# A log-sum-exp kernel on one core: hand-placed semaphores, a four-row first load ahead of the opening barrier, and 18 loads in place of 17

## The chip, the core and the metric

The kernel runs on one core of a Trainium2 chip. The metric is the device time of one execution in microseconds (us). The profile's span, from the program's first instruction to its last, is about 1.8 us shorter than that time. ScalarE, VectorE, GpSimd and SyncE run programs of their own and tell each other of finished work through semaphores, which are counters. At the start and the end of a program all of them wait for each other; these are the opening and the closing barrier. Loads are issued by SyncE and carried out by 16 transfer engines, called "the engines" below where loads are spoken of. A difference in a profile is given in us of the span; a difference between kernels in the runs is given as a ratio, with its us beside it.

## The reference

```python
x = randn(32, 512, 1024).astype(float32)           # axis = -1
x_max = max(x, axis=-1, keepdims=True)
out = x_max.squeeze(-1) + log(sum(exp(x - x_max), axis=-1))    # 32 x 512 float32
```

The input is 67.1 MB. Each of the 16,384 rows of 1,024 numbers gives one number. Both kernels leave the maximum out: with inputs of this size exp does not overflow. The 16,384 rows lie as 128 on each of the 128 partitions, so "a row" below means one row on all 128 partitions, 512 KB.

## The kernel before

A load brings r rows into a ring of 50 row slots. ScalarE takes the exponential in place. The sums go two ways: for the first `n_dve` rows of a load ScalarE takes the exponential in one long instruction and VectorE sums; for the others ScalarE does the row and its sum in one instruction with an accumulator. Logarithms follow in small pieces, and one store ends the kernel. The framework places all semaphores.

```python
CHUNKS = [                                    # (rows, rows summed on VectorE)
    (15, 8), (16, 8), (16, 8), (16, 8), (14, 9), (11, 8), (9, 6), (7, 5), (5, 4),
    (5, 3), (4, 3), (3, 2), (2, 1), (2, 2), (1, 0), (1, 0), (1, 0),
]
RING_ROWS = 50
LN_FROM = 4
# ... cut: pool, tiles, table load ...
    row = slot = logged = 0
    for i, (r, n_dve) in enumerate(CHUNKS):
        if slot + r > RING_ROWS:
            slot = 0
        nc.sync.dma_start(out=ring[:, slot : slot + r], in_=x_v[:, row : row + r])
        if i == len(CHUNKS) - 1:
            take_logs(logged, row)            # a logarithm ahead of the last row
            logged = row
        if n_dve:
            nc.scalar.activation(out=ring[:, slot : slot + n_dve], in_=..., func=Exp)
            nc.vector.reduce_sum(out=sums[:, row : row + n_dve], in_=..., axis=AX)
        for j in range(n_dve, r):
            nc.scalar.activation(out=ring[:, slot + j], in_=..., func=Exp,
                                 accum_out=sums[:, row + j : row + j + 1])
        if r >= LN_FROM:
            take_logs(logged, row)
            logged = row
        slot += r
        row += r
    take_logs(logged, NB)
    nc.scalar.dma_start(out=out_v, in_=res)
```

Loads are numbered from 0 in this text.

The softmax here doesn't subtract the row's maximum and nothing guards it: scores larger than these inputs give would overflow.

Of the kernel before, what the change touches and what calls it, by code (L numbers as in the profile page):

```python
# [1 line left out]

# [4 lines left out]



CHUNKS = [  # L10
    (15, 8), (16, 8), (16, 8), (16, 8), (14, 9), (11, 8), (9, 6), (7, 5), (5, 4),
    (5, 3), (4, 3), (3, 2), (2, 1), (2, 2), (1, 0), (1, 0), (1, 0),
]
RING_ROWS = 50

LN_FROM = 4


@with_exitstack
def kernel(  # L20
    ctx: ExitStack,
    tc: tile.TileContext,
    x: bass.AP,
    axis: bass.AP,
    out: bass.AP,
):
    nc = tc.nc
    P = nc.NUM_PARTITIONS

    assert axis in (-1, len(x.shape) - 1), f"only last-axis reduction supported, got {axis}"  # L30

    x_flat = x.flatten_outer_dims()
    N, D = x_flat.shape
    assert N % P == 0
    NB = N // P
    assert sum(r for r, _ in CHUNKS) == NB

    fp32 = mybir.dt.float32
    Exp = mybir.ActivationFunctionType.Exp
    Ln = mybir.ActivationFunctionType.Ln  # L40
    AX = mybir.AxisListType.X

    x_v = x_flat.rearrange("(p t) d -> p t d", p=P)
    out_v = bass.AP(tensor=out.tensor, offset=out.offset, ap=[[NB, P], [1, NB]])

    pool = ctx.enter_context(tc.tile_pool(name="pool", bufs=1))
    ring = pool.tile([P, RING_ROWS, D], fp32, name="ring")
    sums = pool.tile([P, NB], fp32, name="sums")
    res = pool.tile([P, NB], fp32, name="res")

    nc.scalar.preload_act_table_set("natural_log_exp_and_others")  # L51
    ctx.enter_context(tc.manual_schedule())

    def take_logs(lo, hi):
        if hi > lo:
            nc.scalar.activation(out=res[:, lo:hi], in_=sums[:, lo:hi], func=Ln)  # L56

    row = slot = logged = 0
    for i, (r, n_dve) in enumerate(CHUNKS):
        if slot + r > RING_ROWS:  # L60
            slot = 0
        nc.sync.dma_start(out=ring[:, slot : slot + r], in_=x_v[:, row : row + r])  # L62
        if i == len(CHUNKS) - 1:
            take_logs(logged, row)
            logged = row
        if n_dve:
            nc.scalar.activation(  # L67
                out=ring[:, slot : slot + n_dve], in_=ring[:, slot : slot + n_dve], func=Exp
            )
            nc.vector.reduce_sum(  # L70
                out=sums[:, row : row + n_dve], in_=ring[:, slot : slot + n_dve], axis=AX
            )
        for j in range(n_dve, r):
            nc.scalar.activation(  # L74
                out=ring[:, slot + j],
                in_=ring[:, slot + j],
                func=Exp,
                accum_out=sums[:, row + j : row + j + 1],
            )
        if r >= LN_FROM:  # L80
            take_logs(logged, row)
            logged = row
        slot += r
        row += r

    take_logs(logged, NB)
    nc.scalar.dma_start(out=out_v, in_=res)


# [1 line left out]
_INS = ['x', 'axis']  # L91
_OUTS = [((32, 512), 'float32')]

_NUMBERS = {'axis': -1}


# [26 lines left out]
```

## Time and profile before

The time is 166.47 us (median of 3 runs, 165.97 to 166.50). The profiled run took 166.17 us with a span of 164.4 us.

| what | before |
|---|---|
| first load issued by SyncE | 0.73 us |
| first load (15 rows) landed | 21.88 us |
| reload at the wrap of the ring issued | 57.00 us |
| last load landed | 159.82 us |
| ScalarE starts the last row | 160.51 us |
| store landed | 163.48 us |
| end of the span | 164.40 us |

Landings are times at which the sixteenth transfer engine has raised the load's semaphore, read from the trace's semaphore events.

The profile views in this document show chosen lines word for word; lines between them are left out, also where no dots stand. The view by stretches of the kernel before; the columns are the stretch, its length, busy time of VectorE, ScalarE and GpSimd with counts, granted clock, mean busy share of the 16 transfer engines, and GB/s:

```profile
4.00:60.00 56.00, 17.37 (x2) 29.76 (x33) 0.00 (x0) 1.00 1.01 435
60.00:80.00 20.00, 8.69 (x1) 15.45 (x18) 0.00 (x0) 1.00 0.99 427
80.00:140.00 60.00, 38.86 (x5) 57.09 (x53) 0.00 (x0) 1.00 0.99 426
```

The transfer engines are busy throughout, so the loads bound the middle.

The timeline of the opening of the kernel before (start, duration, engine, line, operation, tiles, count):

```profile
0.33 0.10 POOL L104 MEMSET const-uint8-127<- 128x1 uint8 x1
0.72 1.28 ACT L51 ACT_TABLE_LOAD   x1 [0.72 <-PEq L104]
0.73 1.32 SPq L62 DMA_DIRECT2D ring<-in_x_dram  x3
```

SyncE issues nothing before 0.73 us: until then the opening barrier holds it, GpSimd's constants being the last to finish.

The chain of work that ended last, of the kernel before (start, length, what):

```profile
1.15 40.05 DMA ring<-in_x_dram
...
48.29 8.70 DVE sums L70
...
57.00 0.33 SPq L62
...
57.37 40.16 DMA ring<-in_x_dram
...
158.01 2.30 DVE sums L70
...
160.33 0.02 ACTq L56
```

At 57.00 us SyncE issues reloads as soon as a sum on VectorE releases the slots. At 160.33 us a logarithm on ScalarE was waiting for VectorE's last sum. The timeline of the end of the kernel before:

```profile
158.01 2.29 DVE L70 TENSOR_REDUCE sums<-ring 128x2 f32<-128x2048 f32 x1 [1.14 <-ACT ring L67]
158.92 1.04 ACT L74 ACTIVATE ring<-ring 128x1024 f32<-128x1024 f32 x1
159.87 0.19 ACT L74 ACTIVATION_READ_ACCUMULATOR ring<-ring 128x1 f32 x1
160.39 0.21 ACT L56 ACTIVATE res<-sums 128x13 f32<-128x13 f32 x1 [0.34 <-DVE sums L70]
160.51 1.04 ACT L74 ACTIVATE ring<-ring 128x1024 f32<-128x1024 f32 x1
161.67 0.20 ACT L56 ACTIVATE res<-sums 128x1 f32<-128x1 f32 x1
161.91 0.37 ACTq L87 DMA_DIRECT2D out_dram<-res  x1
```

The last row was in memory at 159.82 us, and ScalarE starts it at 160.51 us, 0.69 us late.

### The profile page before, as it was taken

To read this page: it belongs to the slowest core of one execution; us is meant where nothing else is said; L and a number is where in the kernel's file an instruction comes from. 1 tells how busy PE (TensorE), PEld (TensorE's weight loads), DVE (VectorE), ACT (ScalarE), POOL (GpSimd) and SP (SyncE) were. 2 spreads that over 40 slices of the span, in tenths; PEclk is the share of its full clock that TensorE was granted. 3 is DMA by queue.
4 is the path that set the end of the run, shared out by engine and by line. 5 is a ranking of instruction groups with operands and counts; after the bars stand their busy time and mean duration, and the time that the engine had idled before them with its cause. 6 is when DMAs were issued, how large, how long until landed. Compare 5 with 4: busy or idle time off the path is not lost.

```text
span 164.4 us, 243 instructions
## 1 busy us (share of the span) xinstructions
DVE 82.0 (50%) x14; ACT 124.2 (76%) x133; POOL 0.2 (0%) x4
## 2 busy tenths in 40 slices
DVE  0000000991029800596006940399398979996970
ACT  3000069980999729995399969999989999799993
POOL 0000000000000000000000000000000000000000
DMA  6998999899799979979999989999999999999950
GB/s 239 478 448 389 407 462 510 383 383 510 335 431 510 431 335 494 462 335 496 433 446 433 433 382 428 449 420 431 431 403 433 421 434 424 425 426 416 408 222 16
DMA packets 2593, 67.18 MB, mean 409 GB/s; under 512 B 288, under 2 KB 416, under 8 KB 800
## 3 DMA queue, kind: packets, MB, share of 16 engines
q1 hardware_dynamic: 2448, 67.11, 95.2%
q10 hardware_dynamic: 144, 0.07, 0.1%
q14 instruction: 1, 0.01, 0.0%
HBM read 67.11 MB, written 0.07 MB: 409 GB/s over the span
## 4 chain that ended last, share of the span: by engine, by line
DMA 65%; ACT 18%; DVE 13%; issue 1%; SPq 0%; ACTq 0%
DMA ring<-in_x_dram 65%; ACT ring L67 14%; DVE sums L70 13%; ACT ring L74 4%; SPq L62 0%; ACT res L56 0%; ACTq L56 0%
## 5 line engine op out<-in xcount | busy, mean ns | idle before, releaser
L70 DVE TENSOR_REDUCE sums<-ring 128x8 f32<-128x8192 f32 (+7 forms) x14 | 82.0, 5866 | 78.3 <-ACT ring L67 78.3
L67 ACT ACTIVATE ring<-ring 128x8192 f32<-128x8192 f32 (+7 forms) x14 | 66.8, 4770 | 36.6 <-DMA ring<-in_x_dram 36.5
L74 ACT ACTIVATE ring<-ring 128x1024 f32<-128x1024 f32 x53 | 55.1, 1040 | 0.0
L74 ACT ACTIVATION_READ_ACCUMULATOR ring<-ring 128x1 f32 x53 | 9.9, 187 | 0.0
L56 ACT ACTIVATE res<-sums 128x16 f32<-128x16 f32 (+8 forms) x12 | 2.4, 198 | 0.4 <-DVE sums L70 0.3
L51 ACT ACT_TABLE_LOAD x1 | 1.3, 1283 | 0.7 <-PEq L104 0.7
L104 POOL MEMSET const-bfloat16-1.0<- 128x1 bf16 x1 | 0.1, 102 | 0.0
L104 POOL MEMSET const-uint8-127<- 128x1 uint8 x1 | 0.1, 102 | 0.0
L104 POOL MEMSET const-float32-0.0<- 128x1 f32 x1 | 0.1, 99 | 0.2 <-issue 0.2
L104 POOL MEMSET const-float32-1.0<- 128x1 f32 x1 | 0.1, 99 | 0.0
## 6 DMA issues: line engine op xcount, KB each, us to landing
ring<-in_x_dram SPq DMA_DIRECT2D x1, 7680.0 KB, 21.1
ring<-in_x_dram SPq DMA_DIRECT2D x1, 7168.0 KB, 40.2
ring<-in_x_dram SPq DMA_DIRECT2D x1, 5632.0 KB, 34.3
ring<-in_x_dram SPq DMA_DIRECT2D x2, 2560.0 KB, 33.4
ring<-in_x_dram SPq DMA_DIRECT2D x1, 4608.0 KB, 44.9
ring<-in_x_dram SPq DMA_DIRECT2D x1, 3584.0 KB, 33.9
ring<-in_x_dram SPq DMA_DIRECT2D x1, 2048.0 KB, 31.8
ring<-in_x_dram SPq DMA_DIRECT2D x2, 1024.0 KB, 37.9
```

The costliest lines, as they stand in the source:

```text
L51: nc.scalar.preload_act_table_set("natural_log_exp_and_others")
L56: nc.scalar.activation(out=res[:, lo:hi], in_=sums[:, lo:hi], func=Ln)
L67: nc.scalar.activation(out=ring[:, slot : slot + n_dve], in_=ring[:, slot : slot + n_dve], func=Exp)
L70: nc.vector.reduce_sum(out=sums[:, row : row + n_dve], in_=ring[:, slot : slot + n_dve], axis=AX)
L74: nc.scalar.activation(out=ring[:, slot + j], in_=ring[:, slot + j], func=Exp, accum_out=sums[:, row + j : row + j + 1],)
L104: nc = _bacc.Bacc("TRN2", target_bir_lowering=False, num_devices=1)
```

## The change

Its intent: write the programs of the engines directly, with one semaphore per load, so that the first load can be issued ahead of the opening barrier. With it come a first load of only four rows, another split of the rows, a ring of 51 slots, two logarithms in place of twelve, and GpSimd in place of SyncE as the engine that waits for the store. The core of the diff:

```diff
 CHUNKS = [
-    (15, 8), (16, 8), (16, 8), (16, 8), (14, 9), (11, 8), (9, 6), (7, 5), (5, 4),
-    (5, 3), (4, 3), (3, 2), (2, 1), (2, 2), (1, 0), (1, 0), (1, 0),
+    (4, 0), (16, 10), (14, 13), (15, 4), (16, 7), (15, 6), (12, 9), (9, 6), (7, 5), (5, 4),
+    (4, 3), (3, 3), (2, 2), (2, 0), (1, 1), (1, 0), (1, 0), (1, 0),
 ]
-RING_ROWS = 50
+RING_ROWS = 51
-LN_FROM = 4
+LN_EARLY = 6
 ... (cut: tiles become plain allocations; a semaphore per load, act_done, dve_done, stored)
+    def load(i):
+        (s, row), r = place[i], CHUNKS[i][0]
+        act_wait = max(a for a, _ in busy[s : s + r])
+        dve_wait = max(d for _, d in busy[s : s + r])
+        if dve_wait:
+            nc.sync.wait_ge(dve_done, dve_wait)
+        if act_wait:
+            nc.sync.wait_ge(act_done, act_wait)
+        nc.sync.dma_start(out=ring[:, s : s + r], in_=x_v[:, row : row + r]).then_inc(
+            landed[i], 16
+        )
 ...
+    load(0)
+    n_early = len(body.instructions)
 ...
+        if i == len(CHUNKS) - LN_EARLY:
+            logged = place[i - 1][1]
+            take_logs(0, logged, *done_before[i - 1])
+        nc.scalar.wait_ge(landed[i], 16)
 ... (cut: exponentials and sums as before, each with its increment)
-    take_logs(logged, NB)
-    nc.scalar.dma_start(out=out_v, in_=res)
+    take_logs(logged, NB, dves, acts)
+    nc.scalar.wait_ge(act_done, acts)
+    nc.scalar.dma_start(out=out_v, in_=res).then_inc(stored, 16)
+    nc.gpsimd.wait_ge(stored, 16)
 ...
+    first.instructions = head[:at] + work[:n_early] + head[at:end] + work[n_early:] + head[end:]
```

The last line puts the first load in front of SyncE's part of the barrier (`at`) and the rest behind the barrier.

More of the change, by code (lines that the diff above doesn't have):

```diff
@@ L44 @@
     out_v = bass.AP(tensor=out.tensor, offset=out.offset, ap=[[NB, P], [1, NB]])
-    pool = ctx.enter_context(tc.tile_pool(name="pool", bufs=1))
-    ring = pool.tile([P, RING_ROWS, D], fp32, name="ring")
-    sums = pool.tile([P, NB], fp32, name="sums")
-    res = pool.tile([P, NB], fp32, name="res")
-    nc.scalar.preload_act_table_set("natural_log_exp_and_others")
-    ctx.enter_context(tc.manual_schedule())
-    def take_logs(lo, hi):
-        if hi > lo:
-            nc.scalar.activation(out=res[:, lo:hi], in_=sums[:, lo:hi], func=Ln)
@@ L58 @@
-    row = slot = logged = 0
-    for i, (r, n_dve) in enumerate(CHUNKS):
+    ring = nc.alloc_sbuf_tensor("ring", [P, RING_ROWS, D], fp32).ap()
+    sums = nc.alloc_sbuf_tensor("sums", [P, NB], fp32).ap()
+    res = nc.alloc_sbuf_tensor("res", [P, NB], fp32).ap()
+    landed = [tc.alloc_semaphore(f"landed{i}") for i in range(len(CHUNKS))]
+    act_done = tc.alloc_semaphore("act_done")
+    dve_done = tc.alloc_semaphore("dve_done")
+    stored = tc.alloc_semaphore("stored")
+    hook = nc.pop_inst_callback()
@@ L60 @@
+    symbolic, nc._always_lower_symbolic_ap = nc._always_lower_symbolic_ap, False
+    place = []
+    row = slot = 0
+    for r, _ in CHUNKS:
         if slot + r > RING_ROWS:
             slot = 0
-        nc.sync.dma_start(out=ring[:, slot : slot + r], in_=x_v[:, row : row + r])
-        if i == len(CHUNKS) - 1:
-            take_logs(logged, row)
-            logged = row
+        place.append((slot, row))
+        slot += r
+        row += r
+    busy = [(0, 0)] * RING_ROWS
+    acts = dves = 0
@@ new lines, in load, with take_logs @@
+    def load(i):
[9 more added lines that the diff above has]
+        )
+    def take_logs(lo, hi, dve_wait, act_wait):
+        nonlocal acts
+        nc.scalar.wait_ge(act_done, act_wait)
+        nc.scalar.wait_ge(dve_done, dve_wait)
+        nc.scalar.activation(out=res[:, lo:hi], in_=sums[:, lo:hi], func=Ln).then_inc(
+            act_done, 1
+        )
+        acts += 1
@@ new lines @@
+    body = nc.main_func.blocks[-1]
+    assert not body.instructions
+    load(0)
+    n_early = len(body.instructions)
+    nc.scalar.preload_act_table_set("natural_log_exp_and_others")
+    logged = 0
+    done_before = [(0, 0)]
+    for i, (r, n_dve) in enumerate(CHUNKS):
+        if i:
+            load(i)
+        s, row = place[i]
+        if i == len(CHUNKS) - LN_EARLY:
+            logged = place[i - 1][1]
+            take_logs(0, logged, *done_before[i - 1])
+        nc.scalar.wait_ge(landed[i], 16)
@@ L66 @@
         if n_dve:
             nc.scalar.activation(
-                out=ring[:, slot : slot + n_dve], in_=ring[:, slot : slot + n_dve], func=Exp
-            )
+                out=ring[:, s : s + n_dve], in_=ring[:, s : s + n_dve], func=Exp
+            ).then_inc(act_done, 1)
+            acts += 1
+            nc.vector.wait_ge(act_done, acts)
             nc.vector.reduce_sum(
-                out=sums[:, row : row + n_dve], in_=ring[:, slot : slot + n_dve], axis=AX
-            )
+                out=sums[:, row : row + n_dve], in_=ring[:, s : s + n_dve], axis=AX
+            ).then_inc(dve_done, 1)
@@ L73 @@
+            dves += 1
+            for j in range(n_dve):
+                busy[s + j] = (0, dves)
         for j in range(n_dve, r):
             nc.scalar.activation(
-                out=ring[:, slot + j],
-                in_=ring[:, slot + j],
+                out=ring[:, s + j],
+                in_=ring[:, s + j],
                 func=Exp,
                 accum_out=sums[:, row + j : row + j + 1],
-            )
-        if r >= LN_FROM:
-            take_logs(logged, row)
-            logged = row
@@ L83 @@
-        slot += r
-        row += r
-    take_logs(logged, NB)
-    nc.scalar.dma_start(out=out_v, in_=res)
+            ).then_inc(act_done, 1)
+            acts += 1
+            busy[s + j] = (acts, 0)
+        done_before.append((dves, acts))
+    take_logs(logged, NB, dves, acts)
+    nc.scalar.wait_ge(act_done, acts)
+    nc.scalar.dma_start(out=out_v, in_=res).then_inc(stored, 16)
+    nc.gpsimd.wait_ge(stored, 16)
+    sp = mybir.EngineType.SP
+    first = nc.main_func.blocks[0]
+    head, work = first.instructions, body.instructions
@@ L91 @@
+    at = next(k for k, i in enumerate(head) if i.engine == sp and i.opcode == "Drain")
+    end = next(k for k, i in enumerate(head) if i.opcode == "UnconditionalBranch")
+    first.instructions = head[:at] + work[:n_early] + head[at:end] + work[n_early:] + head[end:]
+    body.instructions = []
+    nc._always_lower_symbolic_ap = symbolic
+    nc.push_inst_callback(hook)
 _INS = ['x', 'axis']
```

## The prediction

> **What bounds the kernel now.** The loads. The page's transfers: 67.11 MB, 95% of the 16 engines' span; by stretches, 435 GB/s from 4 to 60 us and 419 to 427 GB/s from 60 to 156 us. The Trainium skill, "DMA: Bandwidth & Descriptors", section "Where 436 GB/s comes from", gives 435 GB/s as the ceiling of the fabric; this trace agrees: the middle can't shrink. The transfer records fit 1.203 us a row plus about 0.08 us a load (16 rows: 19.32 us; one row: 1.28 us). The two ends are left:
>
> - Front: the first load is issued at 0.73 us, after the opening barrier (SyncE is ready at 0.00 us). First packets follow 1.02 us later; the sixteenth engine starts at 3.40 us. Start-up: 3.0 us in all.
> - Back: the last load lands at 159.82 us. ScalarE is then late: it waited for VectorE's last sum (until 160.30 us), took a logarithm at 160.39 us, and starts the last row at 160.51 us, 0.69 us after landing. Then exponential and accumulator 1.14 us, logarithm 0.2 us, store 1.6 us (161.91 to 163.48 us), SyncE's waits and drains about 0.27 us until GpSimd sees it, closing barrier 0.64 us: 164.4 us. The measured time is about 1.8 us more.
>
> **What the change does.**
>
> 1. First load before the barrier: issue from 0.73 us to near 0.0 us. GpSimd reaches the barrier last (0.53 us), and one issue costs SyncE 0.37 us, so the barrier itself should not move. All landings come about 0.7 us earlier, fully on the critical path. The second load is issued at 0.73 us; the four rows last until about 6 us: no gap.
> 2. 18 loads for 17: +0.08 us.
> 3. Ring and split. With durations of the trace (exponential of n rows 0.853n+0.1 us on ScalarE, row with accumulator 1.039 us, VectorE 1.067n+0.15 us), I estimated the new order by arithmetic. Every reload is released 10 us or more before the queue runs dry (load 4 at about 47 us, needed near 60; load 5 at 70, needed near 80), so no DMA gap. ScalarE is hardly idle from about 100 us on; the early logarithm costs a stop of about 0.9 us at 152 us for VectorE. The last load lands near 159.2 us and ScalarE starts its row about 0.6 us late, much as now. VectorE ends near 159.6 us, no longer last.
> 4. Logarithms 12 to 2: off the path. Separate waits for landings: about 0.05 us each.
> 5. GpSimd waits for the store itself: SyncE's chain goes, about 0.1 us.
>
> Sum: -0.7 +0.08 -0.1, and about -0.1 for the tail's order: -0.8 us.
>
> **Prediction: 165.6 us** (before 166.47), 8 in 10 within 164.8 to 166.3. Faster by over 2%: 0.03; within 2%: 0.95; slower: 0.02.
>
> **What would show it.** Step 1: SyncE's first load issue in the first 0.1 us of the timeline, barrier's end still near 0.65 us, last landing about 159.2 us. Step 3: transfers at 435 GB/s with no gap between 4 and 156 us; ScalarE's last row starting 0.4 to 0.8 us after the last landing. Step 5: under 0.2 us between the store's landing and GpSimd's barrier step.
>
> **What would make it wrong.** The early issue delays the barrier or its packets start later than 1.02 us after it. ScalarE, hardly idle from 100 us, becomes the bound. Reloads that wait for VectorE, whose 13-row sum takes 14 us, could leave the queue empty near 60 or 80 us.

## The result

The kernel after took 164.50 us (median of 4 runs, 164.29 to 164.59) against 166.44 us (median of 4) for the kernel before. The ratio is 0.9888, with a 95% interval of 0.9867 to 0.9908. Ratios in this document are the mean time of one kernel's fast runs over that of the other's of the same rounds, so they are not quite the ratios of the medians quoted. The gain is 1.9 us; 0.8 us was predicted, and the measured time lies below the stated range of 164.8 to 166.3 us.

| what | before | after | difference |
|---|---|---|---|
| first load issued | 0.73 | 0.00 | -0.73 |
| last load landed | 159.82 | 158.51 | -1.31 |
| last row started, after its landing | 0.69 | 0.27 | -0.42 |
| last row's start to the end of the span | 3.89 | 3.97 | +0.08 |
| span | 164.40 | 162.75 | -1.65 |

The view by stretches of the kernel after:

```profile
4.00:60.00 56.00, 15.74 (x2) 31.57 (x24) 0.00 (x0) 1.00 1.02 440
60.00:80.00 20.00, 13.43 (x2) 15.05 (x23) 0.00 (x0) 1.00 0.97 420
80.00:140.00 60.00, 31.85 (x5) 55.61 (x56) 0.00 (x0) 1.00 1.00 430
```

The bytes of these three stretches are within 1% of before's, as they must be when the engines are busy. Bytes are counted where a packet of up to 64 KB starts, so a stretch of 20 us can be off by a few per cent; landings are the finer measure.

The timeline of the opening of the kernel after:

```profile
0.00 2.41 SPq L82 DMA_DIRECT2D ring<-in_x_dram  x4
0.33 0.10 POOL L168 MEMSET const-uint8-127<- 128x1 uint8 x1
0.77 1.28 ACT L100 ACT_TABLE_LOAD   x1 [0.77 <-PEq L168]
```

The first issue now starts the span. The barrier ends 0.05 us later than before (ScalarE's table load moves from 0.72 to 0.77 us).

The chain of work that ended last, of the kernel after:

```profile
1.16 42.58 DMA ring<-in_x_dram
...
69.13 30.69 DMA ring<-in_x_dram
...
99.85 5.32 ACT ring L113
105.17 9.35 ACT ring L125 x18
114.52 7.78 ACT ring L113
...
122.33 29.26 DVE sums L118 x5
...
151.67 0.30 ACT res L90
```

From the landing of load 5 at 99.82 us the chain runs through ScalarE and VectorE, not through transfers. The timeline of its end:

```profile
157.74 1.04 ACT L125 ACTIVATE ring<-ring 128x1024 f32<-128x1024 f32 x1
158.69 0.18 ACT L125 ACTIVATION_READ_ACCUMULATOR ring<-ring 128x1 f32 x1
158.78 1.04 ACT L125 ACTIVATE ring<-ring 128x1024 f32<-128x1024 f32 x1
159.94 0.21 ACT L90 ACTIVATE res<-sums 128x11 f32<-128x11 f32 x1
160.18 0.37 ACTq L137 DMA_DIRECT2D out_dram<-res  x1
```

There is no logarithm between the rows. The last row starts 1.04 us after the one before it, the same pace as the rows with no wait at all, so ScalarE's own pace holds it, 0.27 us behind the landing at 158.51 us. The recorded 1.04 us of one exponential agrees with the Trainium skill, "ScalarE: Activation LUTs", section "What ACT_TABLE_LOAD costs", which gives 186 ns + 0.833 ns an element for an instruction whose scale and bias are immediates: 1039 ns for 1,024 elements. The pace is another matter: in this trace a row without accumulator is followed after 0.95 us (155.75 to 156.70 us), a row with one after 1.04 us.

### The profile page after: what moved, and what is told of

Its sections match the earlier page's. It is cut to its first block, busy times and chain, and to the rows that moved or that the text cites. A ratio compares the mean times of both kernels' runs of the same rounds, so it can differ in the third digit from the quotient of the medians.

```text
span 162.7 us, 208 instructions
## 1 busy us (share of the span) xinstructions
DVE 79.2 (49%) x13; ACT 123.2 (76%) x126; POOL 0.2 (0%) x4
## 4 chain that ended last, share of the span: by engine, by line
DMA 45%; DVE 27%; ACT 26%; issue 0%; SPq 0%; ACTq 0%
DMA ring<-in_x_dram 45%; DVE sums L118 27%; ACT ring L113 17%; ACT ring L125 9%; ACT res L90 0%; SPq L82 0%; ACTq L89 0%
## 5 line engine op out<-in xcount | busy, mean ns | idle before, releaser
L118 DVE TENSOR_REDUCE sums<-ring 128x4 f32<-128x4096 f32 (+9 forms) x13 | 79.2, 6138 | 79.0 <-ACT ring L113 79.0
L113 ACT ACTIVATE ring<-ring 128x4096 f32<-128x4096 f32 (+9 forms) x13 | 64.8, 4987 | 30.3 <-DMA ring<-in_x_dram 30.2
L125 ACT ACTIVATE ring<-ring 128x1024 f32<-128x1024 f32 x55 | 57.2, 1040 | 5.5 <-DMA ring<-in_x_dram 5.5
L90 ACT ACTIVATE res<-sums 128x117 f32<-128x117 f32 (+1 forms) x2 | 0.5, 256 | 0.4 <-DVE sums L118 0.4
```

What stands on the lines that cost most here:

```text
L90: nc.scalar.activation(out=res[:, lo:hi], in_=sums[:, lo:hi], func=Ln).then_inc(act_done, 1)
L113: nc.scalar.activation(out=ring[:, s : s + n_dve], in_=ring[:, s : s + n_dve], func=Exp).then_inc(act_done, 1)
L118: nc.vector.reduce_sum(out=sums[:, row : row + n_dve], in_=ring[:, s : s + n_dve], axis=AX).then_inc(dve_done, 1)
L125: nc.scalar.activation(out=ring[:, s + j], in_=ring[:, s + j], func=Exp, accum_out=sums[:, row + j : row + j + 1],).then_inc(act_done, 1)
```

## The experiments

The theory after the result: the landings came 1.31 us earlier and the tail was 0.42 us shorter because of four separate things, of which the prediction had sized only the first. They are (1) the issue ahead of the barrier; (2) the size of the first load; (3) a reload that the old split issues late at the wrap of the ring; (4) the logarithm that waits for VectorE ahead of the last row. The main rivals are that the programs themselves (without the framework's waits) gave the gain, that start-up shrank because the second issue comes later after the first, that one instruction fetch explains the excess of the landings, and that the new split of the rows gave it.

For the landings I use two derived numbers. "Start-up" is the time from the first issue to the first landing, less 1.203 us a row and 0.08 us. "Excess" is what the later landings take beyond 1.203 us a row and 0.08 us a load. All runs:

| run | ratio to before | first load, rows | issue | start-up | excess | last landing | last row late by |
|---|---|---|---|---|---|---|---|
| before | 1 | 15 | 0.73 | 3.01 | 0.70 | 159.82 | 0.69 |
| a1_own_only | 0.9999 | 15 | 0.73 | 3.12 | 0.81 | 160.04 | 0.72 |
| a2_own_hoist | 0.9960 | 15 | 0.00 | 3.03 | 1.11 | 159.52 | 0.70 |
| a3_own_hoist_small | 0.9935 | 4 | 0.00 | 2.70 | 1.05 | 159.21 | 0.69 |
| a5_wrap_fits | 0.9905 | 5 | 0.00 | 2.61 | 0.30 | 158.37 | 0.67 |
| a4_two_logs | 0.9904 | 4 | 0.00 | 2.42 | 1.20 | 159.08 | 0.19 |
| a6_wrap_and_logs | 0.9867 | 5 | 0.00 | 2.70 | 0.16 | 158.32 | 0.16 |
| after | 0.9888 | 4 | 0.00 | 2.59 | 0.46 | 158.51 | 0.27 |
| u1_load_behind | 0.9920 | 4 | 0.73 | 2.65 | 0.27 | 159.11 | 0.25 |
| u2_sync_waits | 0.9889 | 4 | 0.00 | 2.51 | 0.77 | 158.74 | 0.28 |
| u3_many_logs | 0.9886 | 4 | 0.00 | 2.54 | 0.85 | 158.85 | 0.35 |
| f1_few_scalar | 0.9959 | 4 | 0.00 | 2.59 | 0.12 | 158.17 | 1.77 |
| g1_extra_fetch | 0.9900 | 4 | 0.00 | 2.63 | 0.85 | 158.95 | 0.29 |
| r1_after_again | 0.9869 | 4 | 0.00 | 2.57 | 0.35 | 158.39 | 0.29 |
| r2_a6_again | 0.9870 | 5 | 0.00 | 2.73 | 0.10 | 158.29 | 0.16 |
| a7_last_on_time | 0.9865 | 5 | 0.00 | 2.60 | 0.18 | 158.24 | 0.13 |

The ratios have 95% intervals of 0.0012 to 0.0021 to either side, and each stands against runs of the kernel before on the same chip. The runs lie on several chips (a1 to a3 and u1 on one; a4, a5, u2 and u3 on a second; a6, f1 and g1 on a third; r1, r2 and a7 on a fourth), so a difference of two ratios is uncertain by 0.0018 to 0.003, which is 0.3 to 0.5 us. All results were correct. The other columns are of one profiled run each; the excess varies by a few tenths between runs of one kernel (0.46 and 0.35 for the kernel after). It was worked out with unrounded constants; with 1.203 and 0.08 the column is 0.03 to 0.04 us higher throughout.

### The programs alone, the issue, and the size of the first load

a1 is the kernel after with everything of the old schedule put back, so that only the engine programs, their semaphores and GpSimd's wait for the store remain:

```diff
-    (4, 0), (16, 10), (14, 13), ...
+    (15, 8), (16, 8), (16, 8), ...          # all 17 loads of before; ring of 50
-LN_EARLY = 6                                # and the twelve logarithms of before
+LN_FROM = 4
-    n_early = len(body.instructions)
+    n_early = 0                             # first load behind the barrier
```

> The engine programs with own semaphores alone: old 17 loads, old split, ring of 50, old twelve logarithms, first load behind the barrier; only the wait for the store is GpSimd's. Theory (the gain is made of an earlier issue, a smaller first load and a shorter tail): as the kernel before within 0.2 us, 166.3 us, first landing near 21.9 us, start-up (first issue to first landing, less 1.203 us a row and 0.08 us) 3.0 us. Rival (the programs themselves, without the framework's waits, are worth most of the 1.9 us): 165.3 us or less.

Measured: 166.44 us (166.35 to 166.49), ratio 0.9999. The programs with their own semaphores are worth nothing by themselves; that rival falls.

a2 is a1 with the first load of 15 rows ahead of the barrier.

```diff
-    n_early = 0
+    n_early = len(body.instructions)
```

> a1 with its first load of 15 rows ahead of the barrier. Theory (start-up depends on the size of the first load): issue 0.73 us earlier, start-up still 3.0 us, first landing 21.2 us, time 0.7 us under a1, about 165.6 us. Rival (start-up shrank by 0.4 us because the second issue then comes 0.78 us after the first instead of 0.42 us): start-up 2.6 us, first landing 20.7 us, time 1.1 us under a1.

Measured: 165.87 us (165.54 to 165.96), ratio 0.9960, so 0.65 us under a1. Start-up stayed at 3.03 us although the second issue now came 0.78 us after the first.

a3 is a2 with the first load cut in two.

```diff
-    (15, 8), (16, 8), ...
+    (4, 0), (11, 8), (16, 8), ...
```

> a2 with the first load cut into 4 and 11 rows (18 loads). Theory (size of the first load): start-up 2.6 us, first landing 7.5 us, second landing 0.35 us earlier than a2's first, time 0.3 us under a2, about 165.3 us. Rival (distance of the second issue): start-up as a2's, time as a2's or 0.08 us over.

Measured: 165.43 us (164.86 to 165.84), ratio 0.9935, 0.42 us under a2, with an uncertainty of about 0.4 us. Start-up fell to 2.70 us, and in the two profiles the last landing came 0.31 us earlier.

u1 takes the kernel after and puts only its first load back behind the barrier.

```diff
-    n_early = len(body.instructions)
+    n_early = 0
```

> The kernel after with its first load of four rows back behind the barrier, nothing else changed. Both theories: time 0.7 us over the kernel after, about 165.2 us, as all landings move by 0.73 us. They differ in the start-up: size of the first load says 2.6 us, distance of the second issue (now 0.42 us) says 3.0 us, and then the time is 1.1 us over the kernel after. If ScalarE's and VectorE's work from 100 us on were the bound on its own, not moved by landings, the time would stay at 164.5 us.

Measured: 165.13 us (164.95 to 165.26), ratio 0.9920, which is 0.53 us over the kernel after by its first ratio (0.9888) and 0.85 us by the repeated one (0.9869). Start-up was 2.65 us with the second issue 0.42 us after the first. Together a1, a2, a3 and u1 fill the two-by-two table:

| start-up in us | second issue 0.42 us later | second issue 0.78 us later |
|---|---|---|
| 15 rows | 3.12 (a1) | 3.03 (a2) |
| 4 rows | 2.65 (u1) | 2.59 (after), 2.70 (a3) |

The size of the first load sets the start-up, and the distance of the second issue does not. In the trace the first packets start 1.0 us after the issue in all these runs. With 15 rows the sixteenth engine starts between 1.2 and 1.7 us after the first one, with 4 rows 0.7 to 1.3 us after. These ranges overlap (1.16 us in a1, 1.33 us in u1), so the spread of the starts is not the whole of it. Why the size of the packets (60 KB against 16 KB) matters is not shown.

### The reload at the wrap of the ring

In the old split the first load has 15 rows, and load 3, the first to return to slot 0, has 16. It needs one slot of load 1 as well, and so waits for VectorE's sum of load 1. a5 moves one row, so that 16 slots are exactly two loads:

```diff
-    (4, 0), (11, 8), (16, 8), (16, 8), (16, 8), ...     # a3
+    (5, 0), (11, 8), (15, 8), (16, 8), (16, 8), ...
```

> a3 with one row moved: loads of 5, 11 and 15 rows in place of 4, 11 and 16. The first reload (16 rows, ring slots 0 to 15) then covers only the first two loads, as in the kernel after; in a3 it also covers one row of the third load and so is issued at 56.1 us, 3 us before its engines run dry at 59 us. Theory (a late reload at the wrap of the ring costs the old split 0.4 to 0.8 us, in idle engines and slow first packets near 59 us): reload issued near 38 us, no idle engine at 58 to 60 us, excess of the landings over 1.203 us a row falls from 1.05 us to 0.5 us or less, time 0.4 to 0.6 us under a3's 165.4 us. Rival (the excess is that of one instruction fetch near 74 us, or noise): excess stays near 1 us, time stays at 165.4 us.

Measured: 164.77 us (164.76 to 165.26), ratio 0.9905 against a3's 0.9935, 0.50 us less, with an uncertainty of about 0.4 us. The view of SyncE's issues and the view by stretches of a3:

```profile
56.11 0.80 SPq L82 DMA_DIRECT2D ring<-in_x_dram  x2
```

```profile
57.00:62.00 5.00, 0.00 (x0) 2.33 (x1) 0.00 (x0) 1.00 0.85 354
```

And the same two of a5:

```profile
37.83 18.46 SPq L82 DMA_DIRECT2D ring<-in_x_dram  x2
```

```profile
57.00:62.00 5.00, 0.00 (x0) 2.46 (x1) 0.00 (x0) 1.00 0.97 419
```

The reload is issued at 37.83 us instead of 56.11 us, and in the five microseconds around the wrap the engines are busy 97% instead of 85%. In a3's trace some engines have nothing to do from 58.4 us on, 0.36 us each on average and 1.91 us at most, and several packets there take 0.2 to 0.3 us longer; a5 has neither. The excess falls from 1.05 to 0.30 us.

In the kernel before the reload was issued at 57.00 us, 2.8 us before the first engine had landed its share of the load ahead of it (59.83 us). The view of the same stretch shows nothing of a loss:

```profile
57.00:62.00 5.00, 0.00 (x0) 1.25 (x1) 0.00 (x0) 1.00 1.04 446
```

The idle time there is 0.05 us on average over the 16 engines, but it is nearly all that of one engine, and that engine sets the landings. The trace doesn't name a packet's engine, but an engine's packets nearly always follow each other within 6 ns, so they can be put in rows by their starts. One engine ends its share of load 2 at 60.17 us and starts its share of load 3 only at 60.94 us. Its eight packets of 2.42 us then end at 80.28 us, the last of all, and the load lands at 80.63 us, 0.42 us after the second slowest engine has landed its share. The excess grows by 0.58 us at this load and hardly changes after it. So the late reload costs the landings about half a microsecond in the kernel before as well. The average over 16 engines hides it, because a load lands when its slowest engine does. a1, with the same schedule, shows ten packets near 60 us that took 0.04 to 0.86 us longer, and its excess grows by 0.89 us at that load. So the size of the loss varies from run to run, as the times of a3 do (164.86 to 165.84 us). The kernel after issues its reload at 46.43 us:

```profile
46.43 0.33 SPq L82 DMA_DIRECT2D ring<-in_x_dram  x1
```

The Trainium skill, "DMA: Bandwidth & Descriptors", section "Latency and other measured facts", gives about 0.6 us to the first byte of such a transfer. That agrees with the 1.0 us here, which is counted from the start of an issue of 0.37 us. But 2.6 to 2.8 us of lead is too little: in the kernel before, a1, a2 and a3 the last engine that stood idle got its first packet of the reload 3.4 to 4.2 us after the issue. Why it comes so late is not shown.

### The logarithm ahead of the last row

a4 is a3 with the two logarithms of the kernel after:

```diff
-        if i == len(CHUNKS) - 1:
-            take_logs(logged, row, *done_before[i])
-            logged = row
+        if i == len(CHUNKS) - LN_EARLY:
+            logged = place[i - 1][1]
+            take_logs(0, logged, *done_before[i - 1])
-        if r >= LN_FROM and row > logged:
-            take_logs(logged, row, *done_before[i])
-            logged = row
```

> a3 with the two logarithms of the kernel after in place of twelve, the split as in a3. Theory (ScalarE reaches its last row 0.69 us after landing because the logarithm before it waits for VectorE's last sum): last row starts within 0.1 us of its landing, near 159.3 us, time 0.5 to 0.6 us under a3's 165.4 us. Rival (the shorter tail of the kernel after is due to its split of the last rows): last row still 0.5 us or more after landing, time as a3's.

Measured: 164.89 us (164.75 to 165.02), ratio 0.9904 against a3's 0.9935, 0.52 us less, with an uncertainty of about 0.4 us. The timeline of the end of a4:

```profile
157.32 2.29 DVE L118 TENSOR_REDUCE sums<-ring 128x2 f32<-128x2048 f32 x1 [1.18 <-ACT ring L113]
158.23 1.04 ACT L125 ACTIVATE ring<-ring 128x1024 f32<-128x1024 f32 x1
159.27 1.04 ACT L125 ACTIVATE ring<-ring 128x1024 f32<-128x1024 f32 x1
```

VectorE's last sum still ends at 159.61 us, but no row waits for it: ScalarE starts the last row 0.19 us after its landing at 159.08 us, where a3 was 0.69 us late.

u3 does the reverse: the kernel after with the old rule for logarithms, in its own split.

```diff
-LN_EARLY = 6
+LN_FROM = 4            # the rule of before: after each load of four rows or more, and ahead of the last row
```

> The kernel after with the twelve or so small logarithms of before (one after every load of four rows or more, one ahead of the last row), its own split. Theory (small logarithms hold ScalarE 0.1 us each where it has no idle time, and one stop of 0.41 us near 151.6 us goes): last row starts 0.2 to 0.5 us later, near 159.1 us, time 164.7 to 165.0 us. Rival (the logarithms are off the path): 164.5 us or, for the stop that goes, 164.2 us.

Measured: 164.66 us (164.43 to 164.93), ratio 0.9886: no loss against the first ratio of the kernel after (0.9888), 0.3 us against the repeated one (0.9869), which is within the uncertainty; my number of 164.7 to 165.0 us was a little too high. The last row came 0.35 us after its landing, not 0.5 us or more. In the new split VectorE's last work is a single row followed by three rows of ScalarE alone, so the logarithm ahead of the last row has nothing left to wait for; and the stop of 0.41 us at 151.6 us goes. It still comes between two rows: the last row starts 1.29 us after the row ahead of it (157.91 to 159.20 us) instead of 1.04 us. So most of the cost was not the number of logarithms but one logarithm that waited for a late sum. Either remedy, the two logarithms or the new order of the last rows, removes that wait.

### Who waits for the store

```diff
-    nc.gpsimd.wait_ge(stored, 16)
+    nc.sync.wait_ge(stored, 16)
```

> The kernel after with SyncE in place of GpSimd waiting for the store, nothing else. From the traces: landing of the store to the end of the span was 0.92 us before and 0.98 us after, so GpSimd's wait is worth nothing: 164.5 us within 0.1 us. The prediction's claim was a gain of 0.1 us: 164.6 us and a stretch 0.1 us longer.

Measured: 164.63 us (164.50 to 164.76), ratio 0.9889, the same as the kernel after. From the landing of the store to the end of the span it is 0.92 us before, 0.98 us after and 1.00 us in u2. GpSimd's wait is worth nothing.

### The terms added, and the new split

a6 is a5 with the two logarithms, so it has all four terms but the old split of the later rows.

```diff
-    (4, 0), (16, 10), (14, 13), (15, 4), ...                 # after
+    (5, 0), (11, 8), (15, 8), (16, 8), (16, 8), (14, 9), ...  # then as before; ring of 50
```

> a5 (old split with loads of 5, 11 and 15 rows first, ring of 50) with the two logarithms of the kernel after. If the wrap and the logarithms are separate terms they add: a5 was 0.9905 and a4 0.9904 of before against 0.9935 for a3, so 0.9874, about 164.35 us, as the kernel after (0.9888) or 0.2 us under it, and the new split of the later rows is worth nothing by itself. Rival (the new split is a gain of its own): 0.3 us or more over the kernel after, 164.8 us.

Measured: 164.42 us (164.23 to 164.54), ratio 0.9867. The terms add: 0.9935 for a3, less 0.0030 for the wrap and 0.0031 for the logarithms, is 0.9874. a6 also repeats both steps from the other side: it lies 0.0037 under a4 (the wrap, 0.6 us) and 0.0038 under a5 (the logarithms, 0.6 us). To compare it with the kernel after on one chip I ran both again.

> The kernel after, unchanged, on the same chip as the next two. If its new split of the later rows is worth nothing, it stands within 0.2 us of a6; if it costs something (it stops ScalarE 0.4 us for VectorE near 151.6 us and starts its last row 0.27 us after landing, a6 0.16 us), 0.1 to 0.3 us over a6; if it gains, under it. Its excess of the landings should again be 0.4 to 0.5 us, at load 4, with the fetch near 73 us.

> a6 unchanged, beside the kernel after on one chip: start-up 2.6 us, no idle engine near 59 us, last row 0.1 to 0.3 us after landing, time 0 to 0.3 us under the kernel after.

Measured on one chip: the kernel after 164.33 us (164.03 to 164.44), ratio 0.9869; a6 164.18 us (164.13 to 164.65), ratio 0.9870. They are equal. The new split of the later rows, 18 loads with other shares of VectorE, is worth nothing beyond the wrap and the order of the last rows.

a7 shifts one row of a6 from ScalarE to VectorE:

```diff
-    ... (3, 2), (2, 1), (2, 2), (1, 0), (1, 0), (1, 0),
+    ... (3, 2), (2, 2), (2, 2), (1, 0), (1, 0), (1, 0),
```

> a6 with both rows of the fourteenth load on VectorE in place of one: ScalarE has 0.19 us less work between 145.9 us and the last row, so the last row starts on its landing (within 0.05 us) and the time is 0.1 to 0.2 us under a6. Rival (VectorE, with 1.1 us more, becomes last): last row as in a6 or later, final logarithm waits for VectorE.

Measured: 164.19 us (164.11 to 164.27), ratio 0.9865. The last row is 0.13 us late instead of 0.16 us, so the expectation of 0.05 us was missed, and the time is that of a6. No version here beats the kernel after by more than the noise.

### The instruction fetch

In every trace one packet of 8,192 bytes on the instruction queue (two in g1) falls into the run, mostly between 63 and 77 us, and takes 0.31 us of one transfer engine (0.45 us in f1). In the kernel after the slowest engine's lag behind the second slowest grows from 0.08 us at load 3 to 0.44 us at load 4, during which the fetch comes. Two experiments asked what it costs. f1 gives VectorE all rows of loads 1 to 5, in pieces of at most nine rows, which takes some 67 instructions from ScalarE:

```diff
-    (4, 0), (16, 10), (14, 13), (15, 4), (16, 7), (15, 6), ...
+    (4, 0), (16, 16), (14, 14), (15, 15), (16, 16), (15, 15), ...
+PIECE = 9
 ...
-        if n_dve:
+        for lo in range(0, n_dve, PIECE):
+            n = min(PIECE, n_dve - lo)
 ... (cut: exponential and sum of n rows from s + lo)
```

> The kernel after with all rows of loads 1 to 5 summed on VectorE in pieces of at most nine rows: ScalarE has some 67 instructions fewer and 6.7 us less work before 114 us. Theory (one instruction fetch of 8 KB near 74 us, for ScalarE's stream, delays one of the 16 transfer engines by 0.4 us to the end, and ScalarE's pace, not the landing, sets the last row): no such fetch, or an earlier one; excess of the landings 0.1 us instead of 0.46, last landing near 158.1 us; last row within 0.1 us of it; time 164.0 us. If the fetch stays, last landing 158.5 us, time 164.3 us. If reloads come too late, idle engines near 59, 78 or 111 us show it.

Measured: 166.04 us (165.78 to 166.14), ratio 0.9959: as a kernel it is a failure, and my 164.0 us was wrong. The landings did what was expected: the fetch moved to 160.42 us, the excess fell to 0.12 us and the last load landed at 158.17 us. But VectorE now had more sums than it could finish in time. The chain of the work that ended last, of f1:

```profile
99.50 7.89 ACT ring L116
...
107.41 45.33 DVE sums L121 x7
...
152.83 0.30 ACT res L92
```

VectorE started its last long run of sums at 107.41 us and was not done with the rows of the early logarithm until 152.74 us. ScalarE stood idle for 1.91 us for it (its timeline), and reached the last row 1.77 us after it had landed. The early landing gained nothing, because the end is bound by the two compute engines.

g1 does the opposite: it lengthens ScalarE's stream by 128 tiny exponentials, placed where ScalarE waits for loads 1 and 3.

```diff
+        for k in {1: range(0, 88), 3: range(88, 128)}.get(i, ()):
+            nc.scalar.activation(out=pad_out[:, k : k + 1], in_=pad_in, func=Exp)
         nc.scalar.wait_ge(landed[i], 16)
```

> The kernel after with 128 tiny exponentials of a spare column on ScalarE, 88 where it waits for load 1 and 40 where it waits for load 3, so that its stream is one fetch longer. Theory of the fetch: a second fetch shows on the instruction queue, the same engine is late twice, excess of the landings 0.8 us, last landing near 158.9 us, time 0.2 to 0.4 us over the kernel after. Rival (the fetch is harmless, the late engine has another cause): excess 0.46 us and 164.5 us as before, apart from any row that the tiny exponentials delay.

Measured: 164.99 us (164.78 to 165.27), ratio 0.9900. A second fetch appeared at 18.74 us besides that at 73.73 us, the excess was 0.85 us and the last landing 158.95 us, as expected. The slowest engine landed its share of the last load 0.79 us after the second slowest, and both fetches lie in that engine's row of packets. The excess by itself would not show this: u3, with one fetch, has 0.85 us as well, all of it at load 1, where six packets at 6.8 to 7.1 us took 0.6 to 1.05 us longer. The packets do show it: in every run with a fetch during the loads, the fetch takes 0.31 us, and the packet that starts where it ends takes 0.24 to 0.38 us longer than others of its size. So a fetch costs the engine that carries it 0.55 to 0.69 us. The landing loses less, because that engine was not the last one before: 0.44 us at load 4 in the kernel after, by which the carrier's share lands behind the second slowest. It loses little or nothing where the carrier doesn't become the last alone: in r1, a6 and r2 the two slowest engines end 0.03 to 0.06 us apart in spite of a fetch. In the kernel before the carrier of the fetch ends its share of load 3 at 79.67 us, well before the last engine's 80.28 us; in a1 to a4 it isn't the last engine either. So the fetch is not the excess of the old schedule. It costs the kernel after about 0.44 us of landing that the kernel before doesn't pay, and it explains noise, not the gain. The loss in time is not shown: g1's ratio of 0.9900 can't be told from those of the kernel after (0.9888 and 0.9869).

## Why the prediction was wrong

The prediction's sum was -0.7 + 0.08 - 0.1 - 0.1 = -0.8 us. The runs give, term by term:

- Step 1, the issue ahead of the barrier, -0.7 us: right. It is 0.65 us between a1 and a2 and 0.53 or 0.85 us between u1 and the kernel after. The barrier moved by only 0.05 us.
- "Start-up: 3.0 us in all" was read from a first load of 15 rows and kept for one of four. This is the first mis-sized term. It measured 2.6 us; a3 against a2 shows 0.42 us for it, with the cost of the extra load of step 2 already inside.
- "The middle can't shrink" is the second. The rate of 435 GB/s can't be passed, but the kernel before didn't keep it: the excess of its landings was 0.70 us, and 1.1 us in a2 and a3, which have the same wrap. I had read the reload at 57.00 us in the trace and checked only the new order for lateness, not the old one. Without that late reload, a5 gained 0.50 us. In the kernel before itself 0.58 us of the 0.70 us come at the late reload, on an engine that it left idle and that carries no fetch. The excess of the kernel after is only 0.24 us smaller because there the fetch, which cost the landings of the kernel before nothing, makes its engine the last and adds 0.44 us.
- Step 3's "ScalarE starts its row about 0.6 us late, much as now" is the third. The logarithm that waited for VectorE was described in the prediction and its removal was then put down as "about -0.1". It measured 0.42 us between the profiles and 0.52 us in a4. The arithmetic of the new order was also too slow on VectorE: its formula gives 9.75 us for a sum of nine rows, which is the recorded duration, while in the trace of the kernel after the next sum starts 9.67 us after its start. Five sums in a row stand ahead of the early logarithm. Its stop for VectorE was put at about 0.9 us near 152 us; it took 0.41 us and ended at 151.6 us, part of it through the earlier landings.
- Step 4, the other logarithms and the separate waits: right within the noise, no loss or gain clear of it was seen (a1, u3).
- Step 5, GpSimd's wait, -0.1 us: wrong, it is 0.0 us (u2).

With the four measured terms, 0.65 + 0.42 + 0.50 + 0.52, the sum is 2.1 us, with an uncertainty of about 0.5 us. The kernel after gained 1.9 us in the first comparison and 2.2 us in the second (0.9869), so nothing large is left over. The mechanism of the prediction's step 1 was right; its sum failed because it took two costs of the kernel before for fixed tolls and gave a third, which it had seen, almost no weight.

What stays open: why a small first load has a shorter start-up, why an engine gets its first packet of a late reload up to 4.2 us after the issue, and what decides which engine carries the fetch.

## What to carry to other kernels

When a kernel is bound by its transfers, subtract the ideal landing of every load from the measured one, in the kernel before as well as in the new order: a loss of half a microsecond at one place doesn't show in the busy share, because one idle engine of 16 is enough to delay a landing. A ring should wrap at a border of loads, so that a reload never waits for one slot of a load that is still in use, and a small first load had a shorter start-up here (2.4 to 2.7 us against 3.0 to 3.1 us). A short instruction that waits for another engine, placed ahead of the last piece of work, costs its whole wait, whatever its own length.

## What the Trainium skill lacked or had wrong

- "DMA: Bandwidth & Descriptors", section "Latency and other measured facts", has the first byte but not the start of the sixteenth engine. Here the engines of one load start over 0.7 to 1.7 us, and from the issue to the landing a first load pays 3.0 to 3.1 us beyond its rate with 15 rows a partition and 2.4 to 2.7 us with four.
- The same page, section "Where 436 GB/s comes from": the ceiling of 435 GB/s agrees with the 1.203 us a row here (524,288 bytes in 1.203 us is 436 GB/s). The same section says that for transfers between HBM and SBUF the HBM side, at about 358 GB/s, binds; these loads, on one core, ran at 435 GB/s (4 to 60 us of the kernel before), so here it didn't. The toll of about 0.08 us a load on top, when loads are queued one behind another, is not in that section.
- "Runtime: NRT & Kernel Launch", section "Instruction fetch mechanics", says that instructions are refilled in blocks of 16 KiB (256 instructions) and that the cost is "mostly hidden". Here each fetch in the run is one packet of 8,192 bytes of 0.31 us on a transfer engine, and 128 more instructions brought one more; beside a stream of loads it delayed one engine by 0.55 to 0.69 us, its own 0.31 us and a longer packet after it, and the last landing by a part of that where this engine became the last (g1 against the kernel after: 158.95 against 158.51 us).
- "VectorE: DVE Perf Modes", section "The DRAIN you can't avoid", says that the next operation does not start until the pipe is empty, and adds that one which isn't held starts earlier, without a figure there. In these traces a sum that follows another at once starts 0.04 to 0.09 us before the recorded end of the one ahead, so sums in a row should be costed by their spacing.
